# A hybrid decoder block on Trainium2: two of three split-precision matmuls merged into one of 512 columns

## The chip, the cores and the metric

The kernel runs on one core of one Trainium2 chip. The metric is device time of one execution in microseconds (us); three runs of the kernel before took 468.53, 469.72 and 469.4 us, a median of 469.4 us.

## What is computed

The reference is one decoder layer on 256 tokens of width 1024, all in float32. Cut to its matrix products:

```python
proj = h @ w_in                               # 1024 -> u, v, q, k, vv, q_idx, k_idx, w_idx, g_a, g_b
a_out = spatial_gating(gelu(u), layer_norm(gelu(v)), w_spatial, b_spatial)
b_out = dsa_attention(q, k, vv, q_idx, layer_norm(k_idx), w_idx)    # top 64 keys of each query
mix = sigmoid(g_a) * (a_out @ w_branch_a) + sigmoid(g_b) * (b_out @ w_branch_b)
h = layer_norm(ALPHA * h + mix @ w_o)
gate, val = split(causal_dwconv(h @ w_up, conv_w, conv_b))          # 1024 -> 2 x 2816
h = layer_norm(ALPHA * h + (silu(gate) * val) @ w_down)
```

## The kernel before, in words

**Weights.** All weights are read once, as 75 units of 128 x 2048 floats (1 MB). `prefetch` (line 87) loads a unit into `raw` by a transfer that the SyncE queue issues (line 90), and `split` (lines 74 to 81) divides it: ScalarE writes the high half `hi` (line 77), VectorE the rest, `lo = raw - hi` (line 78), in two pieces of 1024 columns each. `take` (line 102) hands out the next unit and prefetches four ahead; there are three `raw`, five `hi` and five `lo` buffers. The layer's activations are kept as two such halves as well.

**A product** is three matmuls (`mm3`, lines 108 to 111): high x high, high x low and low x high, added up in a PSUM bank; low x low is left out.

**Two kinds of unit.** In `fm_unit` (line 179) the weights are the stationary operand, 128 x 128 at a time, and 256 tokens stream past: 2 column halves x 8 slices of the contraction x 3 matmuls = 48 matmuls of 256 columns, into one bank [128, 2, 256]. Lines 109 and 110 use the same stationary high half, line 111 the low one. Fifty units are of this kind: `qi` (2), `q` (4), `k` (4), the gates `g` (8), `u` (4), the branch products `wb` and `wa` (4 each) and all but the first two of the up projection `up` (20). The others (`vv`, `v`, the output projection `o`, the first two of `up`, the down projection `dn`) hold activations stationary and stream weights, 512 columns in nearly all of them.

**Banks.** PSUM has two pools of four banks. Pool A (`bankA`) is for the units, pool B (`bankB`) for the small products, `o` and `dn`. Whoever reads a unit's bank last frees it for the fourth unit after it.

**Order.** `vv` first, into four banks (line 217), each copied out when its sum is done (line 229). Then `qi`; `q_split` (line 207) turns it into halves. Then `kwb` (line 245), the narrow product of the indexer's keys, copied out by line 246; `kidx_norm` transposes that copy on TensorE from within unit `q0`, at (c, k) = (0, 5) (lines 175 and 252). `indexer_head` and `topk_rounds` (VectorE) choose the keys during `q` and `k`; attention runs head by head between the `g` units. Then `v` with its layer norm, `u`, `spatial` gating, `wb`, `wa` with the merge (lines 448 and 449) and its halves `mh` and `ml` (lines 80 and 81), `o`, the first norm, and eleven up pairs with convolution (`conv_pair`, line 495); from pair 3 on a down unit follows each pair.

**Queues.** Every engine has an order of its own that is fixed when the kernel is built: among the instructions that are ready, the earlier in the program goes first. TensorE, ScalarE, VectorE and the queues of SyncE and GpSimd then run in that order and wait in it.

**Places in SBUF.** `slot(tag)` (line 68) names a place that several tensors use one after the other; a new tensor of a tag waits for the last reader of the old one.

Of the kernel before, what the change touches and what calls it, by code (L numbers as in the profile page):

```python
# [9 lines left out]
F32 = mybir.dt.float32  # L10
# [5 lines left out]
P = 128  # L16
L = 256
# [23 lines left out]
def kernel(  # L41
# [18 lines left out]
    lop = ctx.enter_context(tc.tile_pool(name="lop", bufs=LB))  # L60
    work = ctx.enter_context(tc.tile_pool(name="work", bufs=5))
# [60 lines left out]

    xt_sb = slot("bh", [P, KC, L], name="xt_sb")
    xh = slot("xh", [P, KC, L], F32R, name="xh")
    xl = slot("xl", [P, KC, L], F32R, name="xl")

# [41 lines left out]

    def fm_chunks(hi, lo, mh, ml, bank, hook=None):
# [9 lines left out]
    def fm_unit(name, mh, ml, hook=None):  # L179
        hi, lo = take()  # L180
        bank = bankA([P, 2, L], name)
        fm_chunks(hi, lo, mh, ml, bank, hook)
        return bank

    def tm_pair(name, mh, ml):
        banks = [bankA([P, 512], f"{name}_{t}") for t in range(2)]
# [12 lines left out]
    kThl = const.tile([P, 2, L], F32R, name="kThl")  # L199
    kTh = kThl[:, 0]  # L200
    kTl = kThl[:, 1]
    scr = slot("al", [P, UN], name="scr")
    score = scr[:, 512:896]
# [11 lines left out]

    vv = slot("vv", [P, 2, D], name="vv")
    vbanks = [bankA([P, 512], f"vv{i}") for i in range(4)]
    for kh in range(2):
# [20 lines left out]
    for u in range(2):  # L239
        b = fm_unit(f"qi{u}", xh, xl)  # L240
        q_split(u, b)

    kwb = bankB([72, L], "kwb")
    for k in range(KC):
        mm3(kwb, wkh[:, k, :], wkl[:, k, :], xh[:, k, :], xl[:, k, :], k == 0, k == KC - 1)
    nc.scalar.copy(kwT[0:72, :], kwb)
    widx = const.tile([P, 2, 8], F32, name="widx")

    def kidx_norm():
        kwp = bankB([P, 2, 72], "kwp")  # L250
        for t in range(2):
            nc.tensor.transpose(out=kwp[:, t, :], in_=kwT[0:72, t * P:(t + 1) * P], identity=ident[0:72, 0:72])
        nc.vector.tensor_copy(kw_sb, kwp)
        nc.vector.tensor_scalar(widx, kw_sb[:, :, 64:72], IDX_SCALE, None, op0=ALU.mult)
        for t in range(2):
# [5 lines left out]
            tmp = small.tile([P, 64], F32, tag="ktmp", name=f"ktmp{t}")  # L261
# [42 lines left out]
    for u in range(4):  # L304
        b = fm_unit(f"q{u}", xh, xl, {0: kidx_norm, 2: kidx_transpose}.get(u))
        nc.scalar.copy(qT[:, 2 * u:2 * u + 2, :], b)
        if u > 1:
            for h in range(4 * u - 8, 4 * u - 4):
                indexer_head(h)
    causal_fill(score, NEG)  # L310
    kT = slot("k", [P, 8, L], name="kT")
    for u in range(4):
        b = fm_unit(f"k{u}", xh, xl)
        nc.scalar.copy(kT[:, 2 * u:2 * u + 2, :], b)
        for t in range(2):
            topk_rounds(t, 2 * u, 2 * u + 2)
    make_bias()

    bh = slot("bh", [P, 8, L], F32R, name="bh")
    bl = slot("bl", [P, 8, L], F32R, name="bl")  # L320

# [58 lines left out]
    bs_sb = const.tile([P, D], F32, name="bs_sb")  # L380
    bs = load_par(bs_sb, "bs", nc.sync).rearrange("p (g t) -> p g t", t=P)
# [20 lines left out]

    lnp = slot("al", [P, 2, D], name="lnp")
    lnv_g = load_par(lnp[:, 0], "lnv_g")
# [38 lines left out]
    mh = slot("xh", [P, 8, L], F32R, name="mh")  # L443
    ml = slot("xl", [P, 8, L], F32R, name="ml")
# [114 lines left out]

    up1g = fm_unit("up10", hh, hl, up0_rest)  # L560
    l2p = slot("xl", [P, 2, D], name="l2p")
    ln2_g = load_par(l2p[:, 0], "ln2_g")
    ln2_b = load_par(l2p[:, 1], "ln2_b")

# [141 lines left out]
```

## Time and profile before

| what | us |
|---|---|
| median of three runs | 469.4 |
| the profiled execution, first to last instruction (span) | 466.6 |
| what lies around the span: 469.4 - 466.6 | 2.8 |
| TensorE matmuls busy | 456.6 (98%) |
| VectorE busy | 326.9 (70%) |
| ScalarE busy | 239.8 (51%) |
| TensorE clock granted, mean | 0.996 |

The profiled execution's own time is its span; no other time of it is recorded. A matmul's duration in the profile (283 ns at 256 columns) contains time in which the next one already streams, so what a matmul costs is read from start to start. In the rows below, PE is TensorE, ACT is ScalarE, DVE is VectorE, SPq is SyncE's queue.

### The profile page before, as it was taken

Reading aid. Unit: us, or ns where it says so; the run is one execution under the profiler, and the core shown is the slowest. Engines: PE = TensorE matmul, PEld = TensorE weight load, DVE = VectorE, ACT = ScalarE, POOL = GpSimd, SP = SyncE. Lnnn points to the kernel's source line nnn. Section 1 sums busy time; section 2 is a strip of 40 time slices with the busy share of each in tenths; the row PEclk is TensorE's granted clock in tenths of the full one; section 3 lists DMA queues with packets and bytes.
Section 4 is the critical chain, followed back from the end, with each engine's and each line's share of the span. In section 5 each row is a group of like instructions: output and inputs, shape, how many; then the busy total and the mean of one; then the engine's idle time right before and its main releaser. Section 6 shows DMA issues by size and latency. Waiting matters only on the chain.

```text
span 466.6 us, 7905 instructions
## 1 busy us (share of the span) xinstructions
PE 456.6 (98%) x3278; PEld 429.6 (92%) x3278; DVE 326.9 (70%) x531; ACT 239.8 (51%) x341; POOL 9.5 (2%) x19
## 2 busy tenths in 40 slices
PE   7999999999999999999999999999999999999993
PEld 3799999999999889999998899999999999999983
DVE  3768759946675678486576759998677667667646
ACT  3677644465464567453343238866545545545500
POOL 0001000200000100000000000000000000000000
PEclk9999999999999999999999999999999999999998
DMA  7979762554334644545647057665554454551002
GB/s 230 388 238 376 286 219 107 181 182 180 125 147 166 228 172 157 197 166 195 256 181 266 5 181 280 261 245 202 186 181 180 181 181 180 181 191 81 1 0 91
DMA packets 14995, 86.94 MB, mean 186 GB/s; under 512 B 1648, under 2 KB 2928, under 8 KB 5744
## 3 DMA queue, kind: packets, MB, share of 16 engines
q1 hardware_dynamic: 13536, 81.98, 48.0%
q0 software_dynamic: 1136, 4.19, 2.8%
q8 instruction: 26, 0.43, 0.3%
q10 hardware_dynamic: 288, 0.26, 0.2%
q14 instruction: 9, 0.07, 0.0%
HBM read 85.39 MB, written 1.05 MB: 185 GB/s over the span
## 4 chain that ended last, share of the span: by engine, by line
PE 96%; DMA 1%; DVE 1%; SPq 1%; ACT 0%; issue 0%; DVEq 0%
PE up L111 9%; PE up L110 9%; PE up L109 9%; PE dn L110 4%; PE dn L109 4%; PE dn L111 4%; PE vv L225 4%; PE g L109 3%; PE g L110 3%; PE g L111 3%; PE q L110 2%; PE wa L111 2%; PE wa L110 2%; PE wa L109 2%; PE k L111 2%; PE k L110 2%
## 5 line engine op out<-in xcount | busy, mean ns | idle before, releaser
L78 DVE TENSOR_TENSOR lo<-raw,hi 128x1024 fp32r<-128x1024 f32 (+1 forms) x158 | 181.6, 1166 | 77.1 <-ACT hi L77 77.0
L77 ACT CAST hi<-raw 128x1024 fp32r<-128x1024 f32 (+1 forms) x158 | 155.1, 1005 | 143.2 <-issue 51.7
L109 PE MATMUL up<-hh,hi 128*128 128x256 f32 x320 | 90.7, 283 | 0.0
L111 PE MATMUL up<-hh,lo 128*128 128x256 f32 x320 | 90.6, 283 | 0.0
L110 PE MATMUL up<-hl,hi 128*128 128x256 f32 x320 | 90.6, 283 | 0.0
L110 PEld LDWEIGHTS up<-hl,hi 128*128 128x128 f32 x320 | 61.4, 192 | 0.3
L109 PEld LDWEIGHTS up<-hh,hi 128*128 128x128 f32 x320 | 61.4, 192 | 0.3
L111 PEld LDWEIGHTS up<-hh,lo 128*128 128x128 f32 x320 | 61.4, 192 | 0.0
L109 PE MATMUL g<-xh,hi 128*128 128x256 f32 x128 | 36.9, 288 | 0.0
L111 PE MATMUL g<-xh,lo 128*128 128x256 f32 x128 | 36.2, 283 | 0.0
L110 PE MATMUL g<-xl,hi 128*128 128x256 f32 x128 | 36.2, 283 | 0.0
L110 PE MATMUL dn<-lo,f 128*128 128x512 f32 (+1 forms) x88 | 33.7, 383 | 0.0
L109 PE MATMUL dn<-hi,f 128*128 128x512 f32 (+1 forms) x88 | 33.7, 383 | 0.0
L111 PE MATMUL dn<-hi,f 128*128 128x512 f32 (+1 forms) x88 | 33.6, 382 | 0.0
L506 ACT ACTIVATE y<-up,cv_sb 128x256 f32<-128x256 f32 x40 | 22.4, 563 | 18.7 <-DVE y L509 17.6
L110 PEld LDWEIGHTS g<-xl,hi 128*128 128x128 f32 x128 | 24.5, 192 | 0.0
L109 PEld LDWEIGHTS g<-xh,hi 128*128 128x128 f32 x128 | 24.5, 192 | 0.0
L111 PEld LDWEIGHTS g<-xh,lo 128*128 128x128 f32 x128 | 24.5, 192 | 0.0
L507 DVE SCALAR_TENSOR_TENSOR y<-up,cv_sb,y 128x255 f32<-128x255 f32 x40 | 19.0, 477 | 6.6 <-ACT y L506 6.6
L509 DVE SCALAR_TENSOR_TENSOR y<-up,cv_sb,y 128x254 f32<-128x254 f32 x40 | 19.0, 478 | 0.9
L111 PEld LDWEIGHTS dn<-hi,f 128*128 128x128 f32 x88 | 16.5, 188 | 3.2
L109 PEld LDWEIGHTS dn<-hi,f 128*128 128x128 f32 x88 | 16.6, 188 | 3.1
(204 smaller groups left out, 1024.0 us busy)
## 6 DMA issues: line engine op xcount, KB each, us to landing
raw<-in_wst_dram SPq DMA_DIRECT2D x72, 1024.0 KB, 4.9
raw<-in_wst_dram SPq DMA_DIRECT2D x4, 512.0 KB, 8.8
raw<-in_wst_dram SPq DMA_DIRECT2D x4, 256.0 KB, 4.5
lnp<-in_par_dram POOLq DMA_DIRECT2D x2, 512.0 KB, 6.4
l1p<-in_par_dram POOLq DMA_DIRECT2D x2, 512.0 KB, 6.2
hres<-in_x_dram POOLq DMA_DIRECT2D x1, 1024.0 KB, 5.3
l2p<-in_par_dram POOLq DMA_DIRECT2D x2, 512.0 KB, 4.6
xt_sb<-in_xt_dram SPq DMA_DIRECT2D x4, 128.0 KB, 4.3
```

The costliest lines, as they stand in the source:

```text
L77: a = nc.scalar.copy(hi, src)
L78: return a, nc.vector.tensor_tensor(out=lo, in0=src, in1=hi.bitcast(F32), op=ALU.subtract)
L109: nc.tensor.matmul(ps, ah, bh, start=start, stop=False)
L110: nc.tensor.matmul(ps, ah, bl, start=False, stop=False)
L111: nc.tensor.matmul(ps, al, bh, start=False, stop=stop)
L225: nc.tensor.matmul(vbanks[2 * t + hf], a[:, kk, t * P:(t + 1) * P], b[:, k * 512:k * 512 + 512], start=kk == 0 and n == 0, stop=kk == KC - ...
L506: nc.scalar.activation(y[:, c, :], b[:, c, :], AF.Identity, scale=cv_sb[:, 2, ch:ch + 1], bias=cv_sb[:, 3, ch:ch + 1])
L507: nc.vector.scalar_tensor_tensor(y[:, c, 1:], b[:, c, :L - 1], cv_sb[:, 1, ch:ch + 1], y[:, c, 1:], op0=ALU.mult, op1=ALU.add)
L509: nc.vector.scalar_tensor_tensor(y[:, c, 2:], b[:, c, :L - 2], cv_sb[:, 0, ch:ch + 1], y[:, c, 2:], op0=ALU.mult, op1=ALU.add)
```

## The change

The two halves of an activation lie side by side in one tensor (`x2`, `b2`, `a2`, `m2`, `h2`), so that one matmul streams 256 columns of the high half and 256 of the low half past the same stationary weights. A unit's accumulator is two banks, [128, 2, 2, 256]; `fold` adds the two products. The core of the diff:

```diff
-    psA = ctx.enter_context(tc.tile_pool(name="psA", bufs=4, space=bass.MemoryType.PSUM))
+    psA = ctx.enter_context(tc.tile_pool(name="psA", bufs=2, space=bass.MemoryType.PSUM))
-    xh = slot("xh", [P, KC, L], F32R, name="xh")
-    xl = slot("xl", [P, KC, L], F32R, name="xl")
+    x2 = slot("x2", [P, 2, KC, L], F32R, name="x2")
+    xh, xl = x2[:, 0], x2[:, 1]
+    def mm2(ps, wh, wl, m2k, start, stop):
+        nc.tensor.matmul(ps[:, 0, :], wl, m2k[:, 0], start=start, stop=False, skip_group_check=True)
+        nc.tensor.matmul(ps, wh, m2k, start=False, stop=stop, skip_group_check=True)
-                mm3(bank[:, c, :], wh[:, k, cs], wl[:, k, cs], mh[:, k, :], ml[:, k, :], k == 0, k == KC - 1)
+                mm2(bank[:, c], wh[:, k, cs], wl[:, k, cs], m2[:, :, k, :], k == 0, k == KC - 1)
-        bank = bankA([P, 2, L], name)
+        bank = bankA([P, 2, 2, L], name)
+    def fold(bank, dst=None, name="fold"):
+        if dst is None:
+            dst = work.tile([P, 2, L], F32, tag="w", name=name)
+        nc.scalar.copy(dst, bank[:, :, 1, :])
+        nc.vector.tensor_tensor(out=dst, in0=bank[:, :, 0, :], in1=dst, op=ALU.add)
+        return dst
-    vbanks = [bankA([P, 512], f"vv{i}") for i in range(4)]
+    vpair = [bankA([P, 2, 512], f"vv{t}") for t in range(2)]
+    vbanks = [vpair[i // 2][:, i % 2] for i in range(4)]
-        b = fm_unit(f"qi{u}", xh, xl)
+        b = fold(fm_unit(f"qi{u}", x2), name=f"qif{u}")
         q_split(u, b)
-        mm3(kwb, wkh[:, k, :], wkl[:, k, :], xh[:, k, :], xl[:, k, :], k == 0, k == KC - 1)
-    nc.scalar.copy(kwT[0:72, :], kwb)
+        mm2(kwb, wkh[:, k, :], wkl[:, k, :], x2[:, :, k, :], k == 0, k == KC - 1)
+    nc.scalar.copy(kwT[0:72, :], kwb[:, 1])
+    nc.vector.tensor_tensor(out=kwT[0:72, :], in0=kwb[:, 0], in1=kwT[0:72, :], op=ALU.add)
-        nc.scalar.copy(qT[:, 2 * u:2 * u + 2, :], b)
+        fold(b, qT[:, 2 * u:2 * u + 2, :])
-            nc.scalar.activation(dst[:, 2 * u:2 * u + 2, :], b, AF.Tanh, scale=0.5)
+            gs = fold(b, name=f"gf{g}{u}")
+            nc.scalar.activation(dst[:, 2 * u:2 * u + 2, :], gs, AF.Tanh, scale=0.5)
-    ws_sb = const.tile([P, 8, P], F32, name="ws_sb")
+    ws_sb = slot("ws", [P, 8, P], name="ws_sb")
-        b = fm_unit(f"wa{u}", ah, al)
+        b = fold(fm_unit(f"wa{u}", a2), name=f"waf{u}")
-        conv_pair(i, lambda s: fm_unit(f"up{i}{s}", hh, hl))
+        conv_pair(i, lambda s: fold(fm_unit(f"up{i}{s}", h2), name=f"upf{i}{s}"))
```

`k` goes like `q`; `u`, `wb` and the first up pairs like `wa`. The rest finds places for the wider tensors: `kThl`, `ws_sb` and the last norm's `ln2_g` share one place, `vv` and the indexer's scratch are the two halves of one tensor that `a2` follows, the down projection's inputs `f` are put elsewhere, `up0T` moves to pool B, and the work pool has six buffers instead of five.

## Rows read from the trace of the kernel before

**Rows 1.** The page: busy times, and the granted clock in 40 slices.

```profile
PE 456.6 (98%) x3278; PEld 429.6 (92%) x3278; DVE 326.9 (70%) x531; ACT 239.8 (51%) x341; POOL 9.5 (2%) x19
...
PEclk9999999999999999999999999999999999999998
```

**Rows 2.** The page: shares by engine of the chain that ended last.

```profile
PE 96%; DMA 1%; DVE 1%; SPq 1%; ACT 0%; issue 0%; DVEq 0%
```

**Rows 3.** Groups by line and shape: matmuls of 256 columns in up (busy us, mean ns).

```profile
L110 PE MATMUL up<-hl,hi 128*128 128x256 f32 x320 | 90.6, 283 | 0.0
```

**Rows 4.** Timeline of PE: start us, us, what; into a down unit and out.

```profile
352.18 0.28 PE L111 MATMUL up<-hh,lo 128*128 128x256 f32 x1
352.30 0.40 PE L109 MATMUL dn<-hi,f 128*128 128x512 f32 x1
352.53 0.40 PE L110 MATMUL dn<-lo,f 128*128 128x512 f32 x1
...
353.68 0.39 PE L109 MATMUL dn<-hi,f 128*128 128x512 f32 x1
...
357.54 0.39 PE L111 MATMUL dn<-hi,f 128*128 128x512 f32 x1
357.76 0.28 PE L109 MATMUL up<-hh,hi 128*128 128x256 f32 x1
357.88 0.28 PE L110 MATMUL up<-hl,hi 128*128 128x256 f32 x1
...
369.27 0.40 PE L109 MATMUL dn<-hi,f 128*128 128x512 f32 x1
```

**Rows 5.** Groups by line and shape: readers of a bank.

```profile
L513 DVE TENSOR_TENSOR y<-y,y 128x512 f32<-128x512 f32 x11 | 7.6, 691 | 0.3
L421 DVE TENSOR_TENSOR aw<-sp,bs_sb 128x256 f32<-128x256 f32 x8 | 3.0, 418 | 3.4 <-PE sp L418 3.4
```

**Rows 6.** Timelines of ACT, DVE and PE: end of k1, and start of g02.

```profile
82.66 1.05 ACT L77 CAST hi<-raw 128x1024 fp32r<-128x1024 f32 x1 [3.28 <-PE k L110]
83.61 0.58 ACT L314 COPY kT<-k 128x512 f32<-128x512 f32 x1
...
86.22 1.22 DVE L78 TENSOR_TENSOR lo<-raw,hi 128x1024 fp32r<-128x1024 f32 x1
...
107.17 0.36 PE L109 MATMUL g<-xh,hi 128*128 128x256 f32 x1
```

**Rows 7.** Windows of stage k and early up: length, busy us of PE, PEld, DVE, ACT, POOL.

```profile
71.06:94.09 23.03, 23.03 (x194) 23.03 (x193) 21.29 (x65) 9.72 (x14) 3.18 (x4) 1.00 0.42 142
302.00:318.50 16.50, 16.50 (x139) 16.50 (x138) 15.00 (x23) 9.84 (x16) 0.00 (x0) 1.00 0.56 196
```

**Rows 8.** Timeline of the engines where vv ends and qi begins.

```profile
29.59 1.08 ACT L229 COPY vv<-vv 128x512 f32<-128x512 f32 x2 [0.58 <-PE vv L225]
29.62 0.28 PE L109 MATMUL qi<-xh,hi 128*128 128x256 f32 x1
```

**Rows 9.** Timelines of ACT, DVE and PE: kwb's copy; q0's last matmul before the transposes.

```profile
44.64 0.37 ACT L246 COPY scr<-kwb 72x256 f32<-72x256 f32 x1
...
46.09 0.69 DVE L214 TENSOR_TENSOR qs<-qi,qs 64x512 fp32r<-64x512 f32 x1
...
46.09 0.28 PE L109 MATMUL q<-xh,hi 128*128 128x256 f32 x1
```

**Rows 10.** Timelines of DVE and PE where wa ends and o begins.

```profile
247.93 0.69 DVE L448 SCALAR_TENSOR_TENSOR ga<-ga,wa 128x512 f32<-128x512 f32 x1 [1.45 <-PE wa L111]
...
250.41 0.69 DVE L81 SCALAR_TENSOR_TENSOR ml<-gb,mh 128x512 fp32r<-128x512 f32 x1
...
247.73 0.40 PE L109 MATMUL o<-hi,mh 128*128 128x512 f32 x1
```

**Rows 11.** Timelines of DVE and PE: the last pair's f, and its first user.

```profile
442.04 0.69 DVE L78 TENSOR_TENSOR f<-y,f 128x512 fp32r<-128x512 f32 x1 [0.69 <-ACT f L77]
...
445.38 0.39 PE L109 MATMUL dn<-hi,f 128*128 128x512 f32 x1
```

More of the change, by code (lines that the diff above doesn't have):

```diff
@@ L60 @@
     lop = ctx.enter_context(tc.tile_pool(name="lop", bufs=LB))
-    work = ctx.enter_context(tc.tile_pool(name="work", bufs=5))
+    work = ctx.enter_context(tc.tile_pool(name="work", bufs=6))
     small = ctx.enter_context(tc.tile_pool(name="small", bufs=4))
-    psA = ctx.enter_context(tc.tile_pool(name="psA", bufs=4, space=bass.MemoryType.PSUM))
+    psA = ctx.enter_context(tc.tile_pool(name="psA", bufs=2, space=bass.MemoryType.PSUM))
     psB = ctx.enter_context(tc.tile_pool(name="psB", bufs=4, space=bass.MemoryType.PSUM))
@@ L176, in fm_chunks, with fm_unit @@
                     hook()
-                mm3(bank[:, c, :], wh[:, k, cs], wl[:, k, cs], mh[:, k, :], ml[:, k, :], k == 0, k == KC - 1)
-    def fm_unit(name, mh, ml, hook=None):
+                mm2(bank[:, c], wh[:, k, cs], wl[:, k, cs], m2[:, :, k, :], k == 0, k == KC - 1)
+    def fm_unit(name, m2, hook=None):
         hi, lo = take()
-        bank = bankA([P, 2, L], name)
-        fm_chunks(hi, lo, mh, ml, bank, hook)
-        return bank
+        bank = bankA([P, 2, 2, L], name)
+        fm_chunks(hi, lo, m2, bank, hook)
+        return bank
+    def fold(bank, dst=None, name="fold"):
[4 more added lines that the diff above has]
+        return dst
     def tm_pair(name, mh, ml):
-        banks = [bankA([P, 512], f"{name}_{t}") for t in range(2)]
+        both = bankA([P, 2, 512], name)
+        banks = [both[:, t] for t in range(2)]
         for kh in range(2):
@@ L198 @@
     qs = slot("gb", [P, 8, L], F32R, name="qs")
-    kThl = const.tile([P, 2, L], F32R, name="kThl")
+    kThl = slot("ws", [P, 2, L], F32R, name="kThl")
     kTh = kThl[:, 0]
     kTl = kThl[:, 1]
-    scr = slot("al", [P, UN], name="scr")
+    a2a = slot("a2", [P, 2, UN], name="a2a")
+    scr = a2a[:, 1]
     score = scr[:, 512:896]
@@ L239 @@
     for u in range(2):
-        b = fm_unit(f"qi{u}", xh, xl)
+        b = fold(fm_unit(f"qi{u}", x2), name=f"qif{u}")
         q_split(u, b)
-    kwb = bankB([72, L], "kwb")
+    kwb = bankB([72, 2, L], "kwb")
     for k in range(KC):
-        mm3(kwb, wkh[:, k, :], wkl[:, k, :], xh[:, k, :], xl[:, k, :], k == 0, k == KC - 1)
-    nc.scalar.copy(kwT[0:72, :], kwb)
+        mm2(kwb, wkh[:, k, :], wkl[:, k, :], x2[:, :, k, :], k == 0, k == KC - 1)
+    nc.scalar.copy(kwT[0:72, :], kwb[:, 1])
+    nc.vector.tensor_tensor(out=kwT[0:72, :], in0=kwb[:, 0], in1=kwT[0:72, :], op=ALU.add)
     widx = const.tile([P, 2, 8], F32, name="widx")
@@ L260, in kidx_norm @@
             r = rstd_of(mv, f"k{t}")
-            tmp = small.tile([P, 64], F32, tag="ktmp", name=f"ktmp{t}")
+            tmp = kw_sb[:, t, 0:64]
             nc.vector.tensor_scalar(tmp, kw_sb[:, t, 0:64], mv[:, 0:1], r, op0=ALU.subtract, op1=ALU.mult)
@@ L304 @@
     for u in range(4):
-        b = fm_unit(f"q{u}", xh, xl, {0: kidx_norm, 2: kidx_transpose}.get(u))
-        nc.scalar.copy(qT[:, 2 * u:2 * u + 2, :], b)
+        b = fm_unit(f"q{u}", x2, {0: kidx_norm, 2: kidx_transpose}.get(u))
+        fold(b, qT[:, 2 * u:2 * u + 2, :])
         if u > 1:
@@ L312 @@
     for u in range(4):
-        b = fm_unit(f"k{u}", xh, xl)
-        nc.scalar.copy(kT[:, 2 * u:2 * u + 2, :], b)
+        b = fm_unit(f"k{u}", x2)
+        fold(b, kT[:, 2 * u:2 * u + 2, :])
         for t in range(2):
@@ L317 @@
     make_bias()
-    bh = slot("bh", [P, 8, L], F32R, name="bh")
-    bl = slot("bl", [P, 8, L], F32R, name="bl")
+    b2 = slot("b2", [P, 2, 8, L], F32R, name="b2")
+    bh, bl = b2[:, 0], b2[:, 1]
     pend = {}
@@ L379 @@
                             fill=0.0, base=0, channel_multiplier=-1)
-    bs_sb = const.tile([P, D], F32, name="bs_sb")
+    bs_sb = slot("bs", [P, D], name="bs_sb")
     bs = load_par(bs_sb, "bs", nc.sync).rearrange("p (g t) -> p g t", t=P)
@@ L401, in ln_apply @@
         return nc.vector.scalar_tensor_tensor(dst[:, sl], src[:, sl], r, b[:, sl], op0=ALU.mult, op1=ALU.add)
-    lnp = slot("al", [P, 2, D], name="lnp")
+    lnp = a2a[:, 1].rearrange("p (t d) -> p t d", d=D)
     lnv_g = load_par(lnp[:, 0], "lnv_g")
@@ L408 @@
         ln_apply(vn[:, t], vn[:, t], mv, r, lnv_g, lnv_b)
-    ah = slot("vv", [P, 8, L], F32R, name="ah")
-    al = slot("al", [P, 8, L], F32R, name="al")
+    a2 = slot("a2", [P, 2, 8, L], F32R, name="a2")
+    ah, al = a2[:, 0], a2[:, 1]
     def spatial(j):
@@ L427 @@
     for u in range(4):
-        b = fm_unit(f"u{u}", xh, xl)
+        b = fold(fm_unit(f"u{u}", x2), name=f"uf{u}")
         nc.scalar.activation(uT[:, 2 * u:2 * u + 2, :], b, AF.Gelu_apprx_tanh)
@@ L436 @@
     for u in range(4):
-        b = fm_unit(f"wb{u}", bh, bl)
+        b = fold(fm_unit(f"wb{u}", b2), name=f"wbf{u}")
         us = slice(2 * u, 2 * u + 2)
@@ L441 @@
             spatial(u + 2)
-    mh = slot("xh", [P, 8, L], F32R, name="mh")
-    ml = slot("xl", [P, 8, L], F32R, name="ml")
+    m2 = slot("x2", [P, 2, 8, L], F32R, name="m2")
+    mh, ml = m2[:, 0], m2[:, 1]
     for u in range(4):
-        b = fm_unit(f"wa{u}", ah, al)
+        b = fold(fm_unit(f"wa{u}", a2), name=f"waf{u}")
         us = slice(2 * u, 2 * u + 2)
@@ L459 @@
     ous = [take(0) for _ in range(4)]
-    hh = slot("bh", [P, 8, L], F32R, name="hh")
-    hl = slot("bl", [P, 8, L], F32R, name="hl")
+    h2 = slot("b2", [P, 2, 8, L], F32R, name="h2")
+    hh, hl = h2[:, 0], h2[:, 1]
     st1 = [small.tile([P, 2, 6], F32, tag="st12", name=f"st1_{t}") for t in range(2)]
@@ L489, in h_transpose, with f_slot @@
         return split(hh[:, 4 * j:4 * j + 4, ts], hl[:, 4 * j:4 * j + 4, ts], ps)
-    f_slots = ["q", "vv", "al", "xh", "k", "gb"]
+    f_slots = ["q", ("fa", 0), ("fa", 1), ("fx", 0), ("fx", 1), "k"]
     f_tiles = {}
+    wide = {}
+    def f_slot(j):
+        where = f_slots[j]
+        if isinstance(where, str):
+            return slot(where, [P, 2, 2, 2, L], F32R, name=f"f{j}")
+        tag, half = where
+        if tag not in wide:
+            wide[tag] = slot({"fa": "a2", "fx": "x2"}[tag], [P, 2, 2, 2, 2, L], F32R, name=tag)
+        return wide[tag][:, half]
     dn = []
@@ L496, in conv_pair @@
         if i % 2 == 0:
-            f_tiles[i // 2] = slot(f_slots[i // 2], [P, 2, 2, 2, L], F32R, name=f"f{i // 2}")
+            f_tiles[i // 2] = f_slot(i // 2)
         fh = f_tiles[i // 2][:, i % 2, 0]
@@ L528 @@
     up0 = slot("gb", [P, 2, 2, L], name="up0")
+    up0ps = bankA([P, 2, 2, L], "up0ps")
     up0T = []
@@ L532, in up_first @@
         ts = slice(t * P, (t + 1) * P)
-        bank = bankA([P, 2, L], f"up0_{t}")
+        bank = up0ps[:, t]
         for s in range(2):
@@ L544, in up_first_T @@
         if not up0T:
-            up0T.extend(bankA([P, 2, L], f"up0T{s}") for s in range(2))
+            up0T.extend(bankB([P, 2, L], f"up0T{s}") for s in range(2))
         for s in range(2):
@@ L558, in up0_rest @@
         conv_pair(0, lambda s: up0T[s])
[L560 to L563, printed above, removed]
+    up1g = fm_unit("up10", h2, up0_rest)
+    ln2_g = load_par(slot("ws", [P, D], name="ln2_g"), "ln2_g")
+    ln2_b = load_par(slot("bs", [P, D], name="ln2_b"), "ln2_b")
     def down_mm(bank, t, c, i, unit, w0, w1, start, stop):
@@ L583 @@
         if i == 1:
-            conv_pair(1, lambda s: fm_unit("up11", hh, hl) if s else up1g)
+            conv_pair(1, lambda s: fold(fm_unit("up11", h2) if s else up1g, name=f"upf1{s}"))
         else:
```

8 lines of the change are left out of this document (4 added, 4 removed).

## The prediction

> **What bounds the kernel now.** I read the page's busy times first: TensorE's matmuls cover 98% of the span and the granted clock is full in all slices but the last [rows 1], which is the higher of its two levels, 2.4 GHz. The chain of waits then says whether that is real work or waiting counted as work: 96% of the chain that ended last is TensorE, and no other engine has more than 1% [rows 2]. So a nanosecond taken from TensorE's stream is a nanosecond of time, until another engine makes it wait. The groups by line show what the stream is made of: each of the three lines of a product has 320 matmuls of 256 columns in the 20 `up` units, 16 a unit [rows 3]; over the 50 units that is 800 triples, 2,400 of the 3,278 matmuls [rows 1].
>
> A matmul's price is its step from start to start. Two up units, 96 matmuls, run from 357.76 to 369.27: 0.1199 us each [rows 4], so a triple costs 0.360. In a run of 512 columns a step is (357.54 - 353.68)/17 = 0.227; the first five after 256-column matmuls are longer, (353.68 - 352.30)/6 = 0.230 with the sixth [rows 4]. Twice the columns cost 0.107 more, which is 256 columns at 2.4 GHz; so some 0.013 us of every matmul doesn't grow with its columns. The change can win only that: it streams the same 768 columns per triple in two matmuls instead of three.
>
> **What TensorE gains.** In the new pair, 256- and 512-column matmuls alternate. The trace has each border of this kind: from 352.18 to 352.53 a 256 and a 512 take 0.35, from 357.54 to 357.88 a 512 and a 256 take 0.34 [rows 4]. The deep steps give 0.120 + 0.227 = 0.347. I take 0.3475: the gain is 0.360 - 0.3475 = 0.0122 a triple, x 800 = 9.8 us. The ends: 0.35 gives 8.0 us and 0.34 gives 16; since 0.34 lies below both deep steps and the rows are rounded to 0.01, I cut that end at 0.345, 11.8 us. The 8 triples of `kwb` add 0.1.
>
> Here a rule speaks against the change. The rows' fixed part is 0.013 us. The Trainium skill, "TensorE: Matmul & The Clock Gate", section "Wait — 56ns, not 53.3ns?", puts the fixed part of a warm matmul at about 2.5 ns. By that the change would win 800 x 0.0025 = 2.0 us instead of 9.8. This trace does not agree (0.013 at 256 and at 512 columns), but its matmuls each carry a weight load, and no run here shows alternating widths.
>
> **What is added, and what hides it.** Each of 50 units gets a fold. Its ScalarE copy is 0.58 us, as for `k` [rows 6], and new in 42 units (`q` and `k` had one); its VectorE add of 512 elements is 0.69, and a strided PSUM source adds little (0.418 for 256) [rows 5]. Together 24 us of ScalarE, 34.5 us of VectorE, both off the chain as long as two things hold: the engines have the room, and banks come free in time.
>
> Room. Early up has 15.00 us of VectorE in 16.50; two adds make 16.4 in about 16.1. Stage `k` has 21.29 in 23.03; four adds make 24.1 in about 22.2 [rows 7]. So VectorE runs over by some 2 us in `k` and a little in early up. What waits there first is the weights' low halves, and these are made well ahead: the piece at 86.22 is for `g02`, which TensorE starts at 107.17 [rows 6]. I cost this at 0, end 2.0 for `k` and 0.5 for early up.
>
> Banks. Two accumulators instead of four: a unit must be folded before the one after next begins, that is within one unit, 16 x 0.3475 = 5.6 us. At the end of `k1`, ScalarE first does a piece of `hi` (82.66), then the copy ends at 84.19 [rows 6], some 1.6 us after the unit; a VectorE that is busy with one low half of 1.22 then adds until about 3.5 us. That fits, with 2 us to spare; cost 0. Behind the waiting add on VectorE stand low halves and top-k rounds, both with slack.
>
> Four places have less cover:
> - **vv to qi.** Before, `qi0` started at 29.62 while line 229 still copied the last banks from 29.59 [rows 8]. Now `qi0` needs the accumulator that the first of these two copies frees, at about 30.2: +0.6 us (0.5 to 1.0).
> - **kwb to its transposes.** Before, the copy ended at 45.01 and TensorE came to the transposes at 46.21, 0.12 after the matmul at 46.09, so 1.2 us of cover [rows 9]. Now `kwT` ends with a VectorE add, and VectorE is full there: a `q_split` piece until 46.78 [rows 9], and in front of it the new fold of `qi1` (0.69). The add of 256 (0.42 [rows 5]) ends at about 47.5. TensorE, 0.4 early by its gain and 0.6 late from `vv`, is there by about 46.2: +1.2 us (0 to 2.2). Everything behind the transposes on TensorE waits.
> - **wa to o.** After `wa3`, line 448 started at 247.93 and `ml` was done at 251.10 [rows 10]. `o` first needs the last chunks with its 19th and 20th matmul, 18 x 0.227 = 4.1 us after 247.73, so at 251.8 and 252.05. The fold puts 0.58 + 0.69 and a hand-over ahead: `ml` at about 252.5, less if the copy goes ahead of the `hi` piece: +0.2 us (0 to 1.5).
> - **The last pair.** `f` was done at 442.73, its first user starts at 445.38 [rows 11]; 2.65 us of cover against 1.3 of fold: 0.
>
> `ws_sb` now follows `kThl` in one place, so its load, SyncE's, waits for the last indexer matmul in `q3`; its use comes five stages later, after `u3`, and loads of `raw` behind it are four units ahead: 0. `ln2_g` and `ln2_b` wait for nothing new: 0. `up0T` in pool B, the sixth work buffer, the in-place `tmp`: 0.
>
> **The sum.** 466.6 - 9.8 - 0.1 + 0.6 + 1.2 + 0.2 = 458.7 us of span. The median of the runs is 2.8 above the profiled span, so 461.5 us.
>
> **Rivals.**
> - *A, the accumulators bind.* If the order of ScalarE and VectorE puts the fold behind both halves of a weight unit, the release comes 2 x 1.22 later, around 6 us after the unit's end, and TensorE stops once a unit. It decides from 5.6 us on. For it: VectorE is over its room in `k` and early up [rows 7], and a fold crosses two queues. Against it: before, a piece of `hi` went first and the copy second [rows 6]. At 0.6 us a unit in the 18 units of `k`, `g` and the first up pairs it costs 10.8 us: 461.5 + 10.8 = 472.3, slower.
> - *B, the wide matmul gives nothing back.* Its moving operand lies in two runs of 256, which no row shows. If it streams as two matmuls, at 0.240, the triple stays 0.360; the gain is 0, and the stalls of 2.0 us give 471.4 at most. If instead most of the 0.013 stays with the wider matmul and the gain is only some 2 us, the stalls cancel it: 469.4 - 2.0 + 2.0 = 469.4, no change. Against both: the steps follow 0.107 per 256 columns plus 0.013 at both widths and at both borders [rows 4]. The fixed part that the Trainium skill's page on TensorE, named above, gives would lead to the second form.
> - *C, more stalls than I count.* The upper ends together, 1.0 + 2.2 + 1.5 + 2.0 + 0.5 = 7.2 us with a gain of 8.0: 468.6. Against: they are unlikely to come all together.
>
> **How the numbers follow.** About 0.3% (1.4 us) is what a measurement of this kernel can tell from no change. The forecast, with gains of 8.0 to 11.8 us and stalls of 0.5 to about 5, gets 0.80; it lies between 458 and 466.5 and is faster. A gets 0.10 (slower). B and C together 0.10: 0.08 within 0.3%, 0.01 to each side. So faster 0.81, same 0.08, slower 0.11. The range is 458 to 468: it takes in the forecast's bounds and most of C, and leaves out A and the upper form of B.
>
> **What would show it.** In the changed profile: pairs of 0.345 to 0.35 in the timeline of TensorE in every such unit; up pair plus down unit down from 16.97 us (352.30 to 369.27 [rows 4]) by 32 x 0.0122 to about 16.6; TensorE still over 95% of the chain; a gap of about 0.6 us before `qi0`, about 1 us at the transposes of `kwp`, little before `o`; VectorE near 361 us of busy time and ScalarE near 264. Wrong if pairs take 0.36 (B), or if TensorE has idle time at the start of units, released by a VectorE add (A).

## The result, and the profile after

| | before | after |
|---|---|---|
| median of the runs, us | 468.96 (468.17 to 469.72, 4 runs) | 463.08 (462.89 to 463.18, 4 runs) |
| span of the profiled execution, us | 466.6 | 461.5 |
| matmuls | 3,278 | 2,470 |

The median of before takes in a fourth run (468.17) beside the three that stood ahead of the prediction. The ratio is 0.988, with a 95% interval of 0.986 to 0.990: faster by 1.2%. The forecast was 461.5 us with a range of 458 to 468. The sign and the range hold; several of the terms behind them do not, and they miss in opposite directions.

The page of after, busy times and the shares of the chain that ended last, answering to [rows 1, 2]:

```profile
PE 450.4 (98%) x2470; PEld 385.4 (84%) x2470; DVE 353.2 (77%) x582; ACT 258.9 (56%) x381; POOL 8.2 (2%) x19
...
PE 95%; DMA 1%; DVE 1%; SPq 1%; ACT 0%; issue 0%; DVEq 0%; ACTq 0%
```

TensorE still sets the time. VectorE and ScalarE took on the folds (353 and 259 us; forecast 361 and 264) and are no larger part of the chain. So the result is a matter of how TensorE steps and where it waits.

**How it steps.** The timeline of TensorE in after: the starts of three `wa` units in a row, then of two up units and of the up unit behind the down unit that follows them (start, us, what; the narrow matmul is now line 170, the wide one line 171):

```profile
227.31 0.28 PE L170 MATMUL wa<-a,lo 128*128 128x256 f32 x1
...
232.86 0.28 PE L170 MATMUL wa<-a,lo 128*128 128x256 f32 x1
...
238.41 0.28 PE L170 MATMUL wa<-a,lo 128*128 128x256 f32 x1
...
336.72 0.28 PE L170 MATMUL up<-h,lo 128*128 128x256 f32 x1
...
342.37 0.28 PE L170 MATMUL up<-h,lo 128*128 128x256 f32 x1
...
353.52 0.28 PE L170 MATMUL up<-h,lo 128*128 128x256 f32 x1
```

A unit is 16 pairs. In `wa` it takes 5.55 us, so a pair takes 0.347, the forecast's sum of the two deep steps. In `up` the same unit takes 342.37 - 336.72 = 5.65, a pair 0.353. These are two cadences of the same instructions: a short one, 0.230 + 0.117 in nearly every pair, and a long one, a cycle of three pairs whose wide steps are about 0.233, 0.241 and 0.236. About 28 of the 50 units run in the long one: the four of `k`, the four of `u`, 17 of `up` (all from 298.42 us on) and `q0`, `g00` and `g02`. Summed start to start over all units, the triples of before took 289.1 us and the pairs of after 281.9: a gain of 7.2 us, 0.3524 a pair. An up pair and its down unit went from 16.97 [rows 4] to 353.52 - 336.72 = 16.80; forecast was 16.6.

**Where it waits.** The timeline of TensorE, with the idle time before an instruction and what ended it in brackets; the copies of ScalarE that it waits for follow in the next fence:

```profile
24.63 0.72 PE L239 MATMUL vv<-hi,x 128*128 128x512 f32 x2 [0.45 <-ACT a2a L243]
...
30.83 0.38 PE L170 MATMUL qi<-x,lo 128*128 128x256 f32 x1 [0.45 <-ACT a2a L243]
...
248.70 0.50 PE L109 MATMUL o<-hi,m 128*128 128x512 f32 x1
...
274.08 0.38 PE L109 MATMUL up0ps<-hi,h 128*128 128x256 f32 x1 [0.29 <-ACT up L568]
```

```profile
23.99 1.07 ACT L243 COPY a2a<-vv 128x512 f32<-128x512 f32 x2 [2.19 <-PE vv L239]
...
30.19 1.07 ACT L243 COPY a2a<-vv 128x512 f32<-128x512 f32 x2 [1.31 <-PE vv L239]
...
273.44 0.59 ACT L568 COPY up<-up0ps 128x512 f32<-128x512 f32 x1 [0.55 <-PE up0ps L111]
```

Against the regular step these four cost 0.61, 0.61, 0.2 and 0.46 us, 1.9 together. The second is the forecast wait of `qi0`, the third the forecast one of `o`, which comes when `o` reaches the last chunks. The first and the last were not forecast, and they have one cause: the change makes two banks into one tensor (`vv` of one row half; the first up products `up0ps`), and the matmuls into the second bank now wait until the copy of the first has read it. Before, these were tensors of their own and TensorE went on.

The span fell by 5.1 us. Of 7.2 us of gain, less 1.9 of waits, 0.2 is missing. Summed by product, TensorE's steps show it in `o` (0.1 on the step behind its wait) and in the down units (58.3 us in place of 58.1). The start, where `vv` waits for its weights, took no longer than before but for the two waits, and `kwb` gave 0.04.

### The profile page after: what moved, and what is told of

Read it like the earlier page. It is cut to its first block, busy times and chain, and to the rows that moved or that the text cites. A ratio compares the mean times of both kernels' runs of the same rounds, so it can differ in the third digit from the quotient of the medians.

```text
span 461.5 us, 6329 instructions
## 1 busy us (share of the span) xinstructions
PE 450.4 (98%) x2470; PEld 385.4 (84%) x2470; DVE 353.2 (77%) x582; ACT 258.9 (56%) x381; POOL 8.2 (2%) x19
## 4 chain that ended last, share of the span: by engine, by line
PE 95%; DMA 1%; DVE 1%; SPq 1%; ACT 0%; issue 0%; DVEq 0%; ACTq 0%
PE up L171 16%; PE up L170 8%; PE g L171 6%; PE dn L110 4%; PE dn L111 4%; PE dn L109 4%; PE vv L239 4%; PE g L170 3%; PE k L171 3%; PE u L171 3%; PE q L171 3%; PE wb L171 3%; PE wa L171 3%; PE wa L170 2%; PE wb L170 2%; PE q L170 2%
## 5 line engine op out<-in xcount | busy, mean ns | idle before, releaser
L171 PE MATMUL up<-h,hi 128*128 128x512 f32 x320 | 113.2, 398 | 0.0
L170 PE MATMUL up<-h,lo 128*128 128x256 f32 x320 | 90.0, 281 | 0.0
L171 PEld LDWEIGHTS up<-h,hi 128*128 128x128 f32 x320 | 60.1, 188 | 14.6
L170 PEld LDWEIGHTS up<-h,lo 128*128 128x128 f32 x320 | 60.4, 189 | 0.3
L171 PE MATMUL g<-x,hi 128*128 128x512 f32 x128 | 45.0, 393 | 0.0
L170 PE MATMUL g<-x,lo 128*128 128x256 f32 x128 | 36.5, 286 | 0.0
L171 PEld LDWEIGHTS g<-x,hi 128*128 128x128 f32 x128 | 24.0, 187 | 5.2
L170 PEld LDWEIGHTS g<-x,lo 128*128 128x128 f32 x128 | 24.2, 189 | 0.0
L171 PE MATMUL u<-x,hi 128*128 128x512 f32 x64 | 22.7, 399 | 0.0
L171 PE MATMUL k<-x,hi 128*128 128x512 f32 x64 | 22.7, 399 | 0.0
```

The lines of the kernel that those rows point to most:

```text
L170: nc.tensor.matmul(ps[:, 0, :], wl, m2k[:, 0], start=start, stop=False, skip_group_check=True)
L171: nc.tensor.matmul(ps, wh, m2k, start=False, stop=stop, skip_group_check=True)
```

## The experiments

Each kernel is after with one edit, unless it says otherwise. Ratios are to the kernel before, timed on the same chip (468.5 to 468.7 us in all batches). After was timed in the first batch only, where before took 468.96; a difference to after of less than about 0.5 us can't be told from none.

**1. One matmul back into two.** The wide matmul becomes two of 256 columns; accumulators, folds and order of storage stay.

```diff
-        nc.tensor.matmul(ps, wh, m2k, start=False, stop=stop, skip_group_check=True)
+        nc.tensor.matmul(ps[:, 0, :], wh, m2k[:, 0], start=False, stop=False, skip_group_check=True)
+        nc.tensor.matmul(ps[:, 1, :], wh, m2k[:, 1], start=False, stop=stop, skip_group_check=True)
```

> The merge alone is undone: the high half's two products are two matmuls of 256 columns again, into the same two-bank accumulators, with every fold kept. Theory: the merge gives 7.1 us of TensorE's stream (a pair costs 0.351 instead of a triple of 0.360, 800 times) and everything else of the change costs about 1.9 us, so the stream goes back to 0.120 a step and the time to 469.0 + 1.9 = 470.9 us. Rival: the rest of the change costs nothing, the merge gives only 5.9 us: 469.0. Rival accumulators: if folding into two accumulators held TensorE, units would begin with idle time here too.

Measured: 470.86 us (470.0 to 472.13), ratio 1.005 [1.003, 1.007]. The whole gain is the merge, and without it the change makes the kernel slower: its waits remain, and no unit begins with idle time at a fold. In the profiled execution, which is the slowest of the five (472.13), one wait more appears, at the transposes of `kwp`, where one had been forecast. TensorE, and VectorE and ScalarE before it:

```profile
50.49 0.32 PE L268 MATMUL kwp<-ident,a2a 72*128 72x72 f32 x2 [1.43 <-DVE a2a L262]
```

```profile
49.92 0.42 DVE L262 TENSOR_TENSOR a2a<-kwb,a2a 72x256 f32<-72x256 f32 x1
```

```profile
35.38 2.00 ACT L77 CAST hi<-raw 128x1024 fp32r<-128x1024 f32 x2 [2.16 <-DMA raw<-in_wst_dram]
```

The transposes stand behind twelve triples of `q0` here, as they stand behind twelve pairs in after. What is late is the add: it ends at 50.34, in after at 48.50. ScalarE waited for a load of weights that landed 1.1 us later than in after, and for the next one again, and VectorE's work ran behind it. Whether the other four executions had this wait is not known; the stream alone (289.2 us over the units, without the stop, against 281.9) makes 7.3 us of the 7.8.

**2. Banks as tensors of their own** for `vv` and the first up products, as they were before the change, but with the second column half of `vv` in pool B.

```diff
-    vpair = [bankA([P, 2, 512], f"vv{t}") for t in range(2)]
-    vbanks = [vpair[i // 2][:, i % 2] for i in range(4)]
+    vbanks = [(bankB if i % 2 else bankA)([P, 512], f"vv{i}") for i in range(4)]
-    up0ps = bankA([P, 2, 2, L], "up0ps")
-        bank = up0ps[:, t]
+        bank = bankA([P, 2, L], f"up0_{t}")
```

> The accumulators that are used half by half (vv, and the first up product) are separate tensors again, hf 0 of vv in pool A and hf 1 in pool B. Theory: TensorE's three new waits (0.61 within vv, 0.61 before qi0, 0.46 within the first up product) come from two banks being one tensor, whose second bank waits for the copy of the first; all three go: 463.1 - 1.7 = 461.4 us. Rival: the waits come from where ScalarE's copies stand in its order; then they stay and the time stays at 463.1.

Measured: 461.18 us (460.75 to 461.71), ratio 0.984 [0.983, 0.986], span 459.0. TensorE where `qi` begins, now without a wait:

```profile
28.55 0.62 PE L238 MATMUL vv<-lo,x 128*128 128x512 f32 x2
29.01 0.28 PE L170 MATMUL qi<-x,lo 128*128 128x256 f32 x1
29.12 0.40 PE L171 MATMUL qi<-x,hi 128*128 128x512 f32 x1
```

All three waits (1.7 us) are gone. So the cause is the shared tensor, and the wait of 0.6 at `qi0`, though forecast to size, was not a price of having two accumulators. Some of the 1.9 us has another source: the four units of `k` and three early ones of `up` step by 0.347 here, `qi` and `q3` by 0.353, and the units together take 281.3 us in place of 281.9.

**3. All narrow matmuls of a unit first, then all wide ones.** Same instructions, same operands; they no longer alternate. What is called from within a unit (`hook`, such as the transposes of `kwp`) moves to the end of its narrow matmuls.

```diff
             for k in range(KC):
-                if hook and (c, k) == (0, 5):
+                if hook and (c, k) == (1, 7):
                     hook()
-                mm2(bank[:, c], wh[:, k, cs], wl[:, k, cs], m2[:, :, k, :], k == 0, k == KC - 1)
+                nc.tensor.matmul(bank[:, c, 0, :], wl[:, k, cs], m2[:, 0, k, :], start=k == 0, stop=False,
+                                 skip_group_check=True)
+        for c in range(2):
+            cs = slice(c * P, (c + 1) * P)
+            for k in range(KC):
+                nc.tensor.matmul(bank[:, c], wh[:, k, cs], m2[:, :, k, :], start=False, stop=k == KC - 1,
+                                 skip_group_check=True)
```

> In each unit the 16 narrow matmuls go first, then the 16 wide ones, so widths no longer alternate; same matmuls, same operands. Theory (the price depends on how widths follow each other, with two cadences when they alternate, 0.347 and 0.353 a pair): 16 x 0.120 + 16 x 0.227 + about 0.02 = 5.57 us a unit, 0.348 a pair, in every unit alike; 463.1 - 800 x 0.003 = about 460.7 us. Rival (a wide matmul over two runs of 256 costs 0.234 to 0.236 by itself): 16 x (0.120 + 0.235) = 5.68 a unit; 463.1 + 2.5 = 465.6 us.

Measured: 460.73 us (460.11 to 461.84), ratio 0.983 [0.981, 0.985]. The first five wide steps after narrow ones take 0.229 to 0.236, the others 0.227, with the same moving operand of two runs; the sum over all units is 279.9 us, 2.0 less than in after, and the down units take 0.4 less. So the alternation, not the wide matmul, is what cost more than forecast. A sorted unit takes 5.57 us: less than an alternating one in the long cadence (5.65), but a little more than one in the short (5.55).

**4. The two halves of a slice next to each other**, so that the wide operand is one run of 512.

```diff
-    x2 = slot("x2", [P, 2, KC, L], F32R, name="x2")
-    xh, xl = x2[:, 0], x2[:, 1]
+    x2 = slot("x2", [P, KC, 2, L], F32R, name="x2")
+    xh, xl = x2[:, :, 0], x2[:, :, 1]
```

(`b2`, `a2`, `m2`, `h2` and the slices handed to `mm2` likewise)

> The two halves of each 128-row slice lie next to each other, so that the wide matmul reads one run of 512 instead of two of 256; nothing else. Theory: the two runs cost nothing, the cadence of 0.353 in k, u and up stays: 463.1 us within 0.7. Rival (the two runs make the slow cadence): all pairs at 0.347, 463.1 - 3.1 = 460.0 us.

Measured: 463.74 us (463.06 to 467.18), ratio 0.991 [0.988, 0.994], and the long cadence stands in the same units. The operand's two runs cost nothing.

**5. Experiments 2 and 3 together.**

> The two edits that each helped, together: in a unit first its narrow, then its wide matmuls, and vv's and the first up products' banks as tensors of their own. Theory (the two gains are independent: about 2.4 us of cadence and about 1.7 us of waits for banks that share a tensor): 463.1 - 2.4 - 1.7 = 459.0 us, between 458.5 and 459.7, with no TensorE wait of 0.6 at vv and qi0 and none of 0.46 in the first up product. Rival (what one edit wins is lost again elsewhere, so that they don't add up): 460.5 or more.

Measured: 459.34 us (458.77 to 459.88), ratio 0.980 [0.979, 0.982]. An up unit and the start of the next, in TensorE's timeline:

```profile
333.63 2.08 PE L181 MATMUL up<-h,lo 128*128 128x256 f32 x16
335.55 3.82 PE L186 MATMUL up<-h,hi 128*128 128x512 f32 x16
339.20 2.08 PE L181 MATMUL up<-h,lo 128*128 128x256 f32 x16
```

An up unit takes 339.20 - 333.63 = 5.57 us in place of 5.65. This kernel beats both: 2.0% below before, 0.8% below after. It is 3.7 us faster than after; the two edits alone gave 1.9 and 2.4, but the 0.6 of cadence that experiment 2 held is part of what experiment 3 gives, and counts once.

**6. Every fold made twice**, the second time with the same result.

```diff
-        nc.scalar.copy(dst, bank[:, :, 1, :])
-        nc.vector.tensor_tensor(out=dst, in0=bank[:, :, 0, :], in1=dst, op=ALU.add)
+        for _ in range(2):
+            nc.scalar.copy(dst, bank[:, :, 1, :])
+            nc.vector.tensor_tensor(out=dst, in0=bank[:, :, 0, :], in1=dst, op=ALU.add)
```

> Each fold is made twice over, the second time with the same result: 50 more ScalarE copies of 0.58 us and 50 more VectorE adds of 0.69, and every accumulator comes free about 1.3 us later. Theory (the fold is covered, with 0.5 us to spare at the tightest place, up11's fold before up21, and 2 us or more in k): TensorE stops by about 1 us there and about 1.3 us more between wa and o, perhaps 1 us in k, so 465.5 us, between 464 and 467.5. Rival (the two accumulators are as good as bound, and whatever lengthens the fold is paid in each of the 18 units of k, g and early up): 463 + 18 x 0.7 or more, 475 us.

Measured: 472.04 us (470.03 to 473.84), ratio 1.009 [1.006, 1.012]; the profiled execution has a span of 468.3. Above the theory's 467.5, below the rival's 475. The profiled execution is the fastest of the four. In it TensorE stops not in 18 units; beside the waits of after there are three of more than half a microsecond:

```profile
83.63 0.36 PE L170 MATMUL k<-x,lo 128*128 128x256 f32 x1 [0.54 <-DVE kT L194]
...
265.22 1.21 PE L505 MATMUL hT<-ident,hres 128*128 128x128 f32 x7 [3.20 <-DVE hres L418]
...
298.56 0.36 PE L170 MATMUL up<-h,lo 128*128 128x256 f32 x1 [1.59 <-DVE upf L194]
```

In `k` and early up the fold frees an accumulator too late, as the theory has it. The largest, 3.4 us over the step, lies one stage later than the 1.3 of the theory: not within `o` but behind it, at the transposes of the first norm's output, which VectorE now delivers late. So the cover is real but thin: 50 folds more, some 63 us of added work, cost 8.9 us in the median and 6.8 in this execution, 5.8 of it at these three points, where VectorE is the next to be late. The other three executions show a lower granted clock (0.991 to 0.994 against 0.997); what else slowed them is not known.

**7. The fold's add left out**, the copy kept (a unit's result is then only one of the two sums).

```diff
-        nc.vector.tensor_tensor(out=dst, in0=bank[:, :, 0, :], in1=dst, op=ALU.add)
```

> The fold's VectorE add is left out (the unit's result is then only one of the two products' sums): VectorE has 34.5 us less work and accumulators come free 0.7 us earlier. Theory (the adds are hidden but for some 0.3 us between wa and o and up to 0.6 us around the first up units): 462.5 us, between 461.8 and 463.2. Rival (the missing 2.7 us of the forecast gain are what the adds cost, through VectorE's room): 460.5 us.

Measured: 462.42 us (461.81 to 462.76), ratio 0.987 [0.985, 0.988]. VectorE has 322.2 us to do in place of 353.2, and the time falls by 0.7, little more than can be told from none. The long cadence is in the same units, but for three early up units that have left it and `q1`, which is in it here. The adds are hidden but for the wait of `o` (gone here) and that.

**8. Four matmuls of 128 columns ahead of each up unit.** Their sum is overwritten.

```diff
+        if name.startswith("up"):
+            wl = lo.rearrange("p (k n) -> p k n", n=256)
+            for _ in range(4):
+                nc.tensor.matmul(bank[:, 0, 0, 0:P], wl[:, 0, 0:P], m2[:, 0, 0, 0:P], start=True, stop=False,
+                                 skip_group_check=True)
```

> Four added matmuls of 128 columns at the start of each up unit (their sum is overwritten by the unit's first matmul); they cost about 4 x 0.066 = 0.26 us a unit, 5.3 us over 20 units. Theory (which cadence a unit's alternating pairs fall into is set by what streams just before them; 128-column matmuls lead to the short one): the pairs of the up units after a down unit step by 0.347 instead of 0.353, so 463.1 + 5.3 - 1.9 = 466.5 us. Rival (the cadence goes with the tensors or the stage, not with what came before): 0.353 stays there and the time is 468.4 us.

Measured, one run: 470.75 us. Both expected times miss, because the added matmuls were priced by their columns. TensorE behind a down unit:

```profile
346.18 0.56 PE L189 MATMUL up<-h,lo 128*128 128x128 f32 x4
346.57 0.33 PE L170 MATMUL up<-h,lo 128*128 128x256 f32 x1
346.75 0.40 PE L171 MATMUL up<-h,hi 128*128 128x512 f32 x1
346.98 0.28 PE L170 MATMUL up<-h,lo 128*128 128x256 f32 x1
347.10 0.40 PE L171 MATMUL up<-h,hi 128*128 128x512 f32 x1
347.33 0.28 PE L170 MATMUL up<-h,lo 128*128 128x256 f32 x1
```

Four of them cost (346.57 - 346.18) + 0.06 on the next step = 0.45 us, not 0.26: 9.0 us over 20 units. What the run was made for is in the pairs behind them: 0.35 each, 0.231 + 0.117 in the whole unit, in all 20 up units. With 9.0 added and 17 x 16 x 0.006 = 1.6 taken off, 463.1 becomes 470.5. So the cadence is set by what streams ahead of the unit, not by its tensors or its stage. The other runs bear this out at `up21`: it steps by 0.353 in after, behind four matmuls of `dn`, and by 0.347 in experiments 2 and 7, behind one and none.

**9. The wide matmul first in each pair.**

```diff
-        nc.tensor.matmul(ps[:, 0, :], wl, m2k[:, 0], start=start, stop=False, skip_group_check=True)
-        nc.tensor.matmul(ps, wh, m2k, start=False, stop=stop, skip_group_check=True)
+        nc.tensor.matmul(ps, wh, m2k, start=start, stop=False, skip_group_check=True)
+        nc.tensor.matmul(ps[:, 0, :], wl, m2k[:, 0], start=False, stop=stop, skip_group_check=True)
```

> In each pair the 512-column matmul comes first and the 256-column one second; nothing else differs. Theory (which cadence a run falls into depends on what streams before it, and a unit after a down unit then starts with one more 512-column step): the up units after a down unit still step by 0.353 a pair, 463.1 us, between 462.4 and 463.8. Rival (the long cadence belongs to a run that begins with the narrow matmul): they step by 0.347 and the time is 461.2 us.

Measured: 465.76 us (465.44 to 466.03), ratio 0.994 [0.992, 0.996]: 2.7 slower than after. The rival falls; so does the theory's time. The long cadence holds not only after down units: it is in 40 of the 50 units, `wa`, all of `up` and half of `wb` among them. Twelve pairs of `wa`, which stepped by 0.347 in after:

```profile
228.46 0.40 PE L170 MATMUL wa<-a,hi 128*128 128x512 f32 x1
...
232.70 0.40 PE L170 MATMUL wa<-a,hi 128*128 128x512 f32 x1
```

(232.70 - 228.46)/12 = 0.353. That makes 1.1 us over all units; 0.7 more is a wait behind `o` like that of experiment 6, and the rest lies at the start of `vv`.

**10. The transposes of `kwp` held at their place in the text**, with no matmul of `q0` after the fifth pair, and none of `q1`, ahead of them (the core; the rest hands the last transpose back from `hook`, and `held` on to `q1`).

```diff
-                if hook and (c, k) == (0, 5):
-                    hook()
-                mm2(bank[:, c], wh[:, k, cs], wl[:, k, cs], m2[:, :, k, :], k == 0, k == KC - 1)
+                tr = hook() if hook and (c, k) == (0, 5) else None
+                held = tr or held
+                with tc.issue_after(held.ins) if held else nullcontext():
+                    mm2(bank[:, c], wh[:, k, cs], wl[:, k, cs], m2[:, :, k, :], k == 0, k == KC - 1)
```

> The two transposes of kwp are held at the place that the program's text gives them: no matmul of q0 after the fifth pair, and none of q1, is issued before them. Theory (the predicted stall was avoided only because the fixed order of TensorE put them behind twelve pairs of q0): TensorE reaches them at about 46.6 us, their input is ready at about 48.5, so it stops for 1.9 us and the time is 463.1 + 1.9 = 465.0 us, between 464.3 and 465.7. Rival (the copy and the add are early enough at that place too, or the wait is made good later): no stop over 0.3 us there, 463.1 us.

Measured: 467.22 us (464.41 to 470.65, 10 runs), ratio 0.997 [0.994, 1.000]: 4.1 slower than after, over the theory's 465.7. The profiled execution (468.85 us) shows the stop and what follows it, on TensorE and VectorE:

```profile
46.43 0.40 PE L171 MATMUL q<-x,hi 128*128 128x512 f32 x1
50.26 0.47 PE L271 MATMUL kwp<-ident,a2a 72*128 72x72 f32 x2 [3.43 <-DVE a2a L265]
50.48 0.56 PE L170 MATMUL q<-x,lo 128*128 128x256 f32 x1
50.84 0.63 PE L171 MATMUL q<-x,hi 128*128 128x512 f32 x1
...
55.32 0.51 PE L171 MATMUL q<-x,hi 128*128 128x512 f32 x1
```

```profile
45.27 0.69 DVE L197 TENSOR_TENSOR qif<-qi,qif 128x512 f32<-128x512 f32 x1
45.88 2.35 DVE L78 TENSOR_TENSOR lo<-raw,hi 128x1024 fp32r<-128x1024 f32 x2
48.26 1.40 DVE L231 TENSOR_TENSOR qs<-qif,qs 64x512 fp32r<-64x512 f32 x2
49.69 0.42 DVE L265 TENSOR_TENSOR a2a<-kwb,a2a 72x256 f32<-72x256 f32 x1
```

TensorE stopped for 3.6 us. Here too the add is late: it ended at 50.11, in after at 48.50. VectorE's order at this place is the same as in after; the lateness comes from a load of weights. It was issued at 28.51 (in after at 28.43), but ScalarE got it 1.6 us later. ScalarE in after, then here:

```profile
34.27 2.01 ACT L77 CAST hi<-raw 128x1024 fp32r<-128x1024 f32 x2 [1.10 <-DMA raw<-in_wst_dram]
```

```profile
35.88 2.00 ACT L77 CAST hi<-raw 128x1024 fp32r<-128x1024 f32 x2 [2.64 <-DMA raw<-in_wst_dram]
```

With the load as early as in after, the stop would have been 1.9 (below). And the stop brought a second loss. The windows of this kernel: PE, PEld, DVE, ACT and POOL busy, then the granted clock:

```profile
46.60:50.20 3.60, 0.23 (x1) 0.00 (x0) 3.50 (x6) 3.18 (x5) 0.00 (x0) 0.80 0.88 323
50.20:55.50 5.30, 5.24 (x18) 4.59 (x19) 3.66 (x12) 1.76 (x3) 0.00 (x0) 0.50 0.72 274
55.50:71.00 15.50, 15.50 (x97) 13.80 (x96) 9.30 (x17) 7.95 (x13) 0.00 (x0) 1.00 0.49 173
```

After the idle stretch TensorE ran at half its clock, 1.2 GHz, until about 55.3: seven pairs in 55.32 - 50.84 = 4.48 us, 0.64 a pair in place of 0.347, some 2 us more. The ten runs differ in their granted clock (0.997 in the run of 464.41, 0.989 in that of 470.65), which goes with their spread; the three fastest (464.4 to 464.9, clock 0.995 to 0.998) are within the theory's range. A stop does not always cost the clock: behind the 3.4 us of experiment 6 it stayed at 1.00.

## Why the prediction was right, and where not

**TensorE's gain: right in mechanism, mis-sized.** "I take 0.3475" for a pair: it is 0.347 in about 22 units and 0.353 in about 28, and the gain 7.2 us instead of 9.8, below the lower end of 8.0. The step that failed is the sum of two "deep" steps. It took each width at its own steady step (0.120 and 0.227), and an alternating stream showed neither: in the short cadence the two differences cancel (0.117 + 0.230), so that the sum was right there by luck, and in the long one they don't (0.117 + 0.237 on average). The trace of before held the warning: its border from narrow to wide took 0.35 and the first five wide steps 0.230 [rows 4]. Experiment 3 gives the steady steps back and with them 2.4 us of time. The rule weighed there, the fixed part of about 2.5 ns of the Trainium skill, "TensorE: Matmul & The Clock Gate", section "Wait — 56ns, not 53.3ns?", would have given an estimated 2.0 us. The runs measure 7.2, and had all 50 units stepped as `wa` does (5.76 before, 5.55 after) it would be 10.5, so here the measurement decides against it.

**Rival B** (the wide matmul gives nothing back) falls with experiments 1 and 4: undoing the merge alone costs 7.8 us, 7.3 of it in the stream; the two runs of the operand cost nothing.

**Folds at no cost: right.** VectorE is full in both stages, as worked out. The windows of after for `k` and early up (PE, PEld, DVE and ACT busy), to be held against [rows 7]:

```profile
71.20:93.81 22.61, 22.61 (x130) 19.60 (x129) 22.42 (x65) 9.81 (x14) 2.92 (x3) 1.00 0.50 192
302.00:318.50 16.50, 16.50 (x91) 14.20 (x90) 16.50 (x27) 12.82 (x20) 0.00 (x0) 1.00 0.48 183
```

TensorE is busy throughout both, so the work over VectorE's room fell on what had slack. Leaving the adds out (experiment 7) takes 31 us off VectorE and brings 0.7, so their cost was about that at most.

**Two accumulators at no cost, rival A: right, but closer than the text had it.** No unit of after waits for a fold. The tightest is the fold of `up11`, on VectorE, against the start of `up21`, on TensorE:

```profile
297.25 0.68 DVE L193 TENSOR_TENSOR upf<-up,upf 128x512 f32<-128x512 f32 x1
```

```profile
291.95 0.28 PE L170 MATMUL up<-h,lo 128*128 128x256 f32 x1
...
297.49 1.09 PE L109 MATMUL dn<-hi,f 128*128 128x512 f32 x4
298.42 0.28 PE L170 MATMUL up<-h,lo 128*128 128x256 f32 x1
```

`up11` was done at 291.95 and its fold ends at 297.93, 6.0 us later, where the forecast had 5.6 as the bound and "2 us to spare". It is still 0.5 us ahead of `up21`, but only because four matmuls of `dn` stand in between; without them TensorE would have been there at 297.49. So rival A's condition was met in this one unit, and the built order hid it; the forecast had worked out one place, the end of `k1`, and not this one. Experiment 6 shows the rival's mechanism at work once a fold takes 1.3 us longer, in two units out of 18.

**vv to qi, +0.6: right in size** (0.61), but by a mechanism that the step named only in part. The accumulator is not free because its two banks are one tensor, and that tensor is waited for once more inside `vv`, and once in `up0ps`: 0.61 + 0.46 that the sum lacks. The step looked at who needs a freed accumulator next; it did not look at who writes its other half. Experiment 2 removes all three.

**kwb to its transposes, +1.2: did not come.** TensorE and VectorE in after:

```profile
46.59 0.28 PE L170 MATMUL q<-x,lo 128*128 128x256 f32 x1
...
49.06 0.29 PE L267 MATMUL kwp<-ident,a2a 72*128 72x72 f32 x2
```

```profile
46.65 1.40 DVE L227 TENSOR_TENSOR qs<-qif,qs 64x512 fp32r<-64x512 f32 x2
48.08 0.42 DVE L261 TENSOR_TENSOR a2a<-kwb,a2a 72x256 f32<-72x256 f32 x1
```

The reasoning on VectorE was right, and the add even later than forecast (48.50 against 47.5). But the step took the place of the transposes on TensorE from the text of the kernel, after five pairs of `q0`, that is at 46.59; in the order that was built they stand behind twelve, at 49.06. At the fifth pair TensorE would have stopped for 48.50 - 46.59 = 1.9 us. Experiment 10 shows the stop where the order doesn't avoid it (3.6 us, 1.6 of it from the late load). Experiment 1 shows that the order's cover of 0.56 us is thin: behind the same twelve, a late load alone brought a stop of 1.6.

**wa to o, +0.2: right** (0.17 at the wait, 0.11 on the step behind it). **The last pair, 0: right**; no wait there.

**The sum.** Against a span of 458.7: +2.6 for the gain, +1.1 for the two waits unseen, -1.2 for the one that didn't come, +0.1 for `o`, +0.2 for the down units, gives 461.5. The median lies 1.6 above this span, not 2.8, and so 463.1. The term of 2.8 was mis-sized too: it set the span of one run against the times of others, and in every run with both on record the time is 1.7 to 2.0 above the span. The forecast of 461.5 was missed by 1.6 us, and came that near because the errors partly cancel, which is luck.

**Left open:** why an alternating stream has two cadences, and what in the stream ahead picks one. That it is the stream ahead is shown (experiment 8); the mechanism is not. It is more than the last few matmuls: `k0` follows the same sixteen matmuls of `rel` in after and in experiment 2, and steps by 0.354 in one and 0.347 in the other; `q3`, ahead of these sixteen, stepped by 0.347 and 0.353.

## What to carry to other kernels

Merging matmuls that share a stationary operand pays by the part of a step that doesn't grow with its columns (here 0.013 us of each matmul taken away, of which 0.009 came through), but price a mixed stream by its borders, not by each width's steady step, and where it falls into a long cadence try the matmuls of one width together. When banks are joined into one tensor, look for every writer of one half while another engine still reads the other. And take an instruction's place from the order that was built, since an order that fills waits with other ready work can make a late input free, and a change of that order, or a load that lands later, can make it dear.

## What the runs showed of the hardware that was not expected

- The same pairs of 256 and 512 columns stepped at 0.347 or 0.353 us, and stayed in one of the two for whole units; with four matmuls of 128 columns ahead all 20 up units ran in the short one (3 did without), and the wide matmul first put 40 of the 50 units into the long one.
- A matmul of 128 columns, each with a weight load, took 0.11 us (0.45 for four), nearly as much as one of 256 (0.120).
- After a stop of 3.6 us the granted clock was 0.50 for about 5 us, so that the stop cost about half as much again behind it.
- Loads of the same weight unit, issued within 0.1 us of each other, reached ScalarE at 34.27, 35.38 and 35.88 us in three executions.
